# Rotating 96 planes by 180 degrees: all transfers on one DMA ring, in 8 MB pieces

The program runs on one core of a Trainium2 chip. The metric is the device time of one execution in microseconds (us), as a median of several executions; the other core of the pair is idle, so every bandwidth below is that of a single core.

Some words first. HBM is the main memory, in which input and output lie; SBUF is the core's working memory. A DMA transfer moves data between them, or within one of them, and is cut into packets. A ring is the queue in which the transfers of one issuing engine wait for the DMA engines. A transfer has landed when its last semaphore record is in.

## The reference

```python
def setup_inputs():
    batch, c, h, w = 32, 3, 256, 256
    return {"x": np.random.randn(batch, c, h, w).astype(np.float32)}

def reference(x):
    return np.rot90(x, k=2, axes=(-2, -1)).astype(np.float32)
```

Each of the 96 planes of 256 x 256 floats is read backwards, element by element. 25.17 MB come in, 25.17 MB go out, and nothing is computed.

## The kernel before

The planes are worked on in three groups of 32. In a group each plane is cut into four rows of 64 KB, so a group fills a tile of 128 partitions x 64 KB, 8.39 MB. VectorE reverses the elements within a row; the store reverses the order of the four rows (`::-1`). Three tiles of 64 KB per partition are in use: groups 0 and 2 are loaded to A and reversed into Ct, group 1 is loaded to Bt and reversed in place with the help of T.

```python
def load(t, g, lo=0, hi=E):
    nc.sync.dma_start(out=t[:, lo:hi], in_=x4[g][:, lo:hi])

def store(t, g):
    for lo in (0, E // 2):
        nc.scalar.dma_start(out=o4[g][:, ::-1, lo:lo + E // 2],
                            in_=t[:, lo:lo + E // 2])
...
load(A, 0)
load(Bt, 1)
across(Ct, A)      # 4 copies, 8.9 us
store(Ct, 0)
load(A, 2)
inside(Bt)         # 12 copies, 15.1 us
store(Bt, 1)
across(Ct, A)
store(Ct, 2)
```

SyncE (SP) issues the loads and ScalarE (ACT) the stores, so there are two rings of DMA work, and the 16 DMA engines serve both.

## Time and profile before

| | before |
|---|---|
| device time, median of 3 | 123.26 us |
| profiled execution | 123.51 us, span 121.7 us |
| VectorE busy | 32.5 us (27%) |
| DMA engines busy, SP's ring and ACT's ring | 49.3% + 47.9% |
| bytes over the span | 50.33 MB, 413 GB/s |

The lines themselves stand in the prediction. A share of "16 engines" is the sum of the durations of the packets that *start* in the stretch asked for, over 16 times the length of the stretch; in a short stretch it may pass 100%. The time of one packet follows by dividing.

### The profile page before, as it was taken

To read this page: it belongs to the slowest core of one execution; us is meant where nothing else is said; L and a number is where in the kernel's file an instruction comes from. 1 tells how busy PE (TensorE), PEld (TensorE's weight loads), DVE (VectorE), ACT (ScalarE), POOL (GpSimd) and SP (SyncE) were. 2 spreads that over 40 slices of the span, in tenths; PEclk is the share of its full clock that TensorE was granted. 3 is DMA by queue.
4 is the path that set the end of the run, shared out by engine and by line. 5 is a ranking of instruction groups with operands and counts; after the bars stand their busy time and mean duration, and the time that the engine had idled before them with its cause. 6 is when DMAs were issued, how large, how long until landed. Compare 5 with 4: busy or idle time off the path is not lost.

```text
span 121.7 us, 78 instructions
## 1 busy us (share of the span) xinstructions
DVE 32.5 (27%) x20; POOL 0.2 (0%) x4
## 2 busy tenths in 40 slices
DVE  0000000599400000699992000199700000000000
POOL 0000000000000000000000000000000000000000
DMA  9779977998978999899998996999898989999992
GB/s 345 345 345 495 538 345 345 560 474 345 345 301 388 485 441 431 366 485 441 452 409 388 517 452 301 463 398 485 377 485 388 485 377 485 398 463 409 452 431 108
DMA packets 1296, 50.33 MB, mean 413 GB/s; under 512 B 144, under 2 KB 144, under 8 KB 144
## 3 DMA queue, kind: packets, MB, share of 16 engines
q1 hardware_dynamic: 432, 25.17, 49.3%
q10 hardware_dynamic: 864, 25.17, 47.9%
HBM read 25.17 MB, written 25.17 MB: 413 GB/s over the span
## 4 chain that ended last, share of the span: by engine, by line
DMA 57%; DVE 13%; DVEq 2%; issue 0%
DMA A<-in_x_dram 57%; DVE Ct L53 13%; DVEq L108 2%; DVEq L53 0%
## 5 line engine op out<-in xcount | busy, mean ns | idle before, releaser
L53 DVE COPY Ct<-A 128x4096 f32<-128x4096 f32 x8 | 17.8, 2288 | 36.8 <-DMA A<-in_x_dram 36.8
L53 DVE COPY T<-Bt 128x2048 f32<-128x2048 f32 x4 | 4.9, 1228 | 18.0 <-DMA Bt<-in_x_dram 17.9
L53 DVE COPY Bt<-T 128x2048 f32<-128x2048 f32 x4 | 4.9, 1227 | 0.1
L53 DVE COPY Bt<-Bt 128x2048 f32<-128x2048 f32 x4 | 4.9, 1226 | 0.1
L97 POOL MEMSET const-uint8-127<- 128x1 uint8 x1 | 0.1, 102 | 0.0
L97 POOL MEMSET const-bfloat16-1.0<- 128x1 bf16 x1 | 0.1, 101 | 0.0
L97 POOL MEMSET const-float32-0.0<- 128x1 f32 x1 | 0.1, 98 | 0.2 <-issue 0.2
L97 POOL MEMSET const-float32-1.0<- 128x1 f32 x1 | 0.1, 98 | 0.0
## 6 DMA issues: line engine op xcount, KB each, us to landing
out_dram<-Ct ACTq DMA_DIRECT2D x4, 4096.0 KB, 34.2
out_dram<-Bt ACTq DMA_DIRECT2D x2, 4096.0 KB, 32.6
A<-in_x_dram SPq DMA_DIRECT2D x2, 34.5
Bt<-in_x_dram SPq DMA_DIRECT2D x1, 48.4
```

Source lines behind the costliest of these rows:

```text
L53: tc.keep_in_program_order(nc.vector.tensor_copy(out=dst, in_=src))
L97: nc = _bacc.Bacc("TRN2", target_bir_lowering=False, num_devices=1)
L108: with _tile.TileContext(nc) as tc:
```

## The change

Its intent: no competition between the rings. Loads and stores go through SP's ring alone, in the order load, load, store, load, store, store, and every transfer is one of 8 MB in 64 KB packets, half as many store packets as before.

```diff
     def store(t, g):
-        for lo in (0, E // 2):
-            nc.scalar.dma_start(out=o4[g][:, ::-1, lo:lo + E // 2],
-                                in_=t[:, lo:lo + E // 2])
+        nc.sync.dma_start(out=o4[g][:, ::-1, :], in_=t[:, :])
```

## The prediction

> **What bounds the kernel now.** I read the page first (engines, DMA row, queues, chain), then the issues in order of time, then the queue lines of three stretches, and last the packet records of the trace one by one. The page:
>
> ```profile
> DVE 32.5 (27%) x20; POOL 0.2 (0%) x4
> ...
> DMA  9779977998978999899998996999898989999992
> ...
> DMA packets 1296, 50.33 MB, mean 413 GB/s; under 512 B 144, under 2 KB 144, under 8 KB 144
> ...
> q1 hardware_dynamic: 432, 25.17, 49.3%
> q10 hardware_dynamic: 864, 25.17, 47.9%
> ...
> DMA A<-in_x_dram 57%; DVE Ct L53 13%; DVEq L108 2%; DVEq L53 0%
> ```
>
> VectorE works 27% of the span, the DMA engines 49.3 + 47.9 = 97.2%. q1 is SP's ring with the loads (25.17 MB in 64 KB packets), q10 is ACT's with the stores (25.17 MB in 32 KB packets); the small packets are semaphore writes. The chain of waits names a load for 57% and VectorE for 13%, but it stops at VectorE's last copy, at 87.6 us. The 34 us after that are stores draining, which the chain does not follow. So I trust the queue lines and not the chain: the bound is the 16 DMA engines, and the question is how many microseconds of them are not spent at full pace.
>
> The issues in order of time (start, length, engine, what):
>
> ```profile
> 0.73 0.37 SPq L56 DMA_DIRECT2D A<-in_x_dram  x1
> 1.15 0.42 SPq L56 DMA_DIRECT2D Bt<-in_x_dram  x1
> 22.80 8.90 DVE L53 COPY Ct<-A 128x4096 f32<-128x4096 f32 x4 [22.80 <-DMA A<-in_x_dram]
> 27.32 4.96 ACTq L60 DMA_DIRECT2D out_dram<-Ct  x2
> 31.72 0.33 SPq L56 DMA_DIRECT2D A<-in_x_dram  x1
> 49.61 1.23 DVE L53 COPY T<-Bt 128x2048 f32<-128x2048 f32 x1 [17.91 <-DMA Bt<-in_x_dram]
> ```
>
> From 27.3 us on both rings hold work, and each takes a share: the second load lands only at 49.6 and the third at 78.6 us (landing 46.9 us after its issue), against 22.0 us for the first, which had the engines alone.
>
> Queue lines of three stretches, 29 to 37 us, 37 to 77 us, and 80 to 118 us (name: packets, MB, share of 16 engines' time):
>
> ```profile
> q1 hardware_dynamic: 40, 2.62, 92.8%
> q10 hardware_dynamic: 20, 0.66, 19.0%
> ```
> ```profile
> q1 hardware_dynamic: 192, 10.88, 62.8%
> q10 hardware_dynamic: 203, 6.13, 35.5%
> ```
> ```profile
> q10 hardware_dynamic: 568, 16.52, 100.6%
> ```
>
> Divide time by packets. In the mixed stretch 10.88 MB are 166 load packets; 62.8% of 16 x 40 us is 401.9 us, so 2.42 us each (27.1 GB/s an engine, 434 GB/s for 16). 6.13 MB are 187 store packets of 1.21 us each, the same pace. Stores alone, third stretch: 504 packets in 611.6 us, 1.21 us again. The packet records agree: median 2.418 us for 64 KB and 1.213 us for 32 KB, whether the other ring runs or not. Only the first stretch differs: 40 load packets share 118.8 us, 2.97 us each. Loads and stores together cost nothing; the *arrival* of the stores at 29 us does. Summed over the records, load packets begun from 29 to 37 us take 1.38 us per engine beyond the median, those begun before 4 us (the very first) 0.57 us, all later ones 0.
>
> **What the Trainium skill says.** "DMA: Bandwidth & Descriptors", section "Issuing engines are not separate DMA queues": DMAs started by different engines run on the same 16 DMA engines and interleave; using several issuers saves only issue time. The trace agrees: 434 GB/s with one ring and with two, and an issue takes 0.33 to 0.62 us. The same page, section "Queues, rings and completion order": each engine takes turns between the rings that have work, a packet at a time. Agrees: a 64 KB load packet against a 32 KB store packet would share engine time 2 to 1, and the mixed stretch has 62.8 to 35.5. "Where 436 GB/s comes from", same page, gives 435 GB/s as the ceiling of the 16 ports; the records' 434 is that, so no order of transfers can raise the steady pace. "HBM Reference", section "Latency", gives an HBM access of 0.2 us on average and 2 us at high load; no row here isolates it, and I use it only for the size of one rival below.
>
> **The change part by part.**
>
> 1. *ACT issues nothing; six 4 MB stores become three 8 MB stores of 64 KB packets.* If a 64 KB store packet takes what a 64 KB load packet takes, 2.418 us, then 24 of them per engine (384 over 16) take 24 x 2.418 = 58.03 us, against 48 x 1.213 = 58.22 us now: 0.19 us saved. Fewer semaphore packets (9 ns each in the records, three fewer per engine): 0.03 us, neglected.
>
> 2. *One ring, strictly in order: load 0, load 1, store 0, load 2, store 1, store 2.* Each is 8 packets per engine, 8 x 2.418 = 19.34 us. Load 0 lands at 22.8 as now. Then load 1 at 42.1, store 0 at 61.5, load 2 at 80.8, store 1 at 100.1, store 2 at 119.5. I must check that each is in the ring before the ring runs dry. Store 0 is issued when the copy ends at 31.7 (now its first half goes at 27.3; SP has to wait for all of it); load 2 right after, at about 32.3: both before 42.1. Load 1 lands 7.5 us earlier than now, and the in-place reversal (12 copies, 49.61 to 64.7, so 15.1 us) runs from 42.2 to 57.3; store 1 is issued then, before the ring empties at 80.8. Load 2 lands at 80.8, Ct has been free since 61.5, the copies (8.9 us) end at 89.8; store 2 is issued at about 90, ten microseconds before 100.1. The ring never empties after 1.7 us, and all 32.5 us of VectorE stay hidden. SP's waits are in the order in which they come true, so no load is held behind a store that could have gone first in a harmful way.
>
> 3. *The end.* Now the last store lands at 120.94 (semaphore records) and the span ends 0.79 us later. Replayed with full-pace packets from load 0's landing, today's kernel would end at 22.77 + 16 x 2.418 + 48 x 1.213 = 119.68; it ends at 120.94, so 1.26 us on the slowest engine are the disturbance at 29 to 37 us. With the change and no disturbance: 22.77 + 40 x 2.418 = 119.49, span 120.28. Saving 1.26 + 0.19 = 1.45 us. The timed runs lie 123.26 - 121.73 = 1.53 us above the span, which I keep: 121.8 us at best.
>
> **The rivals.**
>
> *A. The disturbance belongs to waking a second ring.* For: it occurs when ACT's ring gets its first work, the very first packets on SP's ring also run long (2.69 to 3.47 us for most), and the issues at 63.5, 64.7, 83.2 and 87.6 us, which find a ring still filled, show no long packet. Then it goes with the second ring: 121.8 us.
>
> *B. It belongs to the first stores of the run, whichever ring carries them.* For: the same moment is also the first write to HBM. Then it returns at about 41 us: 121.8 + 1.3 = 123.1 us. The trace cannot separate A and B; I give A 60%.
>
> *C. One ring pays for every change of direction.* With two rings an engine switches between load and store at nearly every packet at no cost, which speaks against it. But each ring may read ahead while the other writes; in one ring, a load behind a store might first have to fetch. There are three changes of direction. If each stalls for a latency between the skill's 0.2 and 2 us, an estimate from that page, it is 0.6 to 6 us; with the free switching seen I expect 0.1 us each, 0.3 in sum.
>
> *D. SP's strict order starves the ring.* Part 2 leaves 9 to 23 us of room at every issue, so this needs an error of 9 us in my schedule: hardly possible.
>
> *E. The earlier landing of loads 1 and 2 speeds the kernel.* Load 1 does land 7 us earlier, but nothing that ends late waits for it: worth 0.
>
> **Range and chances.** 121.8 + 0.4 x 1.3 (B) + 0.3 (C) = 122.6; C may well be zero, so I put 122.4 us, 0.7% faster than 123.26. Low end 121.5: A, and a slightly better start. High end 123.5: B, with some of C. Faster by over 2% means under 120.8, a span under 119.3; even the 48 packets per engine at 2.418 us (116.06) plus the first packet's start at 1.73 and the 0.79 at the end give 118.6, without the long first packets and the spread of the engines. That needs an error in the packet time: 3%. Slower by over 2% means over 125.7, so 4 us of stalls that only C at its upper size gives: 4%. Within 2%: 93%.
>
> **What would show each step.** The queue line of the page should have one ring with about 50.33 MB, about 97 to 98% of the engines' span, and no q10; the packets fall to some 864 (768 of 64 KB and 96 semaphore writes). Landings near 22.8, 42, 61.5, 81, 100 and 119.5 us prove the FIFO schedule; steps clearly over 19.4 us show where the loss is. Rival B shows as long packets around 41 us; C as idle engines or long packets at 41, 61 and 80 us alike; D as an issue on SP after its predecessor has landed. VectorE's first copy of the in-place reversal should start near 42 instead of 49.6 us. I am wrong if 64 KB store packets take more than 2.42 us, if direction changes stall, or if the end after the last landing grows.

## The result

| | before | after |
|---|---|---|
| device time, median | 123.24 us (4 runs, 123.02 to 123.27) | 123.14 us (4 runs, 123.04 to 123.27) |
| ratio, 95% interval | | 0.9997 (0.998 to 1.0014) |
| span of the profiled execution | 121.73 us | 121.26 us |

A ratio is the mean time of one kernel's fast runs over that of the other's of the same rounds, so not quite the ratio of these medians. The change made no difference that can be told from zero; a later repetition of five rounds (below) says the same.

The page of the changed kernel, with the lines that answer to those of before:

```profile
DVE 32.5 (27%) x20; POOL 0.2 (0%) x4
...
DMA packets 864, 50.33 MB, mean 415 GB/s; under 512 B 96, under 2 KB 96, under 8 KB 96
...
q1 hardware_dynamic: 864, 50.33, 97.3%
```

One ring, 864 packets, 97.3% of the engines' time: as busy as before. The issues and copies in order of time (start, length, engine, what, and in brackets what VectorE waited for):

```profile
22.57 8.90 DVE L53 COPY Ct<-A 128x4096 f32<-128x4096 f32 x4 [22.57 <-DMA A<-in_x_dram]
31.50 0.63 SPq L59 DMA_DIRECT2D out_dram<-Ct  x1
32.17 0.59 SPq L56 DMA_DIRECT2D A<-in_x_dram  x1
43.09 1.23 DVE L53 COPY T<-Bt 128x2048 f32<-128x2048 f32 x1 [11.62 <-DMA Bt<-in_x_dram]
...
58.22 0.55 SPq L59 DMA_DIRECT2D out_dram<-Bt  x1
81.94 8.90 DVE L53 COPY Ct<-A 128x4096 f32<-128x4096 f32 x4 [23.74 <-DMA A<-in_x_dram]
90.86 0.54 SPq L59 DMA_DIRECT2D out_dram<-Ct  x1
```

The schedule is the foretold one, an issue always well before its turn. From the semaphore records, the six transfers land at 22.55, 43.07, 62.60, 81.84, 101.17 and 120.46 us. The steps between them are 20.5, 19.5, 19.2, 19.3 and 19.3 us: all are the 8 x 2.418 = 19.34 us of eight full-pace packets, but for the first, which is 1.2 us too long. Where those 1.2 us are, the queue line of two stretches of 2 us shows, 38.5 to 40.5 us (the last packet of load 1 on each engine) and 77.5 to 79.5 us (the last packet of load 2):

```profile
q1 hardware_dynamic: 16, 1.05, 177.1%
...
q1 hardware_dynamic: 16, 1.05, 121.5%
```

With 16 packets begun in 2 us, one on each engine, the mean packet is the share times 2 us: 3.54 us in the first stretch, 2.43 us in the second. 120.9% would be the undisturbed 2.418 us. So the last load packet before store 0 takes 1.12 us more, on all 16 engines (0.89 to 1.55 in the packet records), and the last one before store 1, which also goes from loading to storing, takes what any packet takes. I call these 1.1 us the toll. (The records do not name the engine of a packet; but the end of one packet is the start of the next, and so they fall into 16 rows of equal length.) In the kernel before it was 1.38 us: ten engines lost 1.1 to 1.4 us in the load packet ahead of their first store packet, six lost 0.6 to 0.8 us there and another 0.7 to 1.1 us in the next load packet.

### The profile page after: what moved, and what is told of

Read it like the earlier page. It is cut to its first block, busy times and chain, and to the rows that moved or that the text cites. A ratio compares the mean times of both kernels' runs of the same rounds, so it can differ in the third digit from the quotient of the medians.

```text
span 121.3 us, 72 instructions
## 1 busy us (share of the span) xinstructions
DVE 32.5 (27%) x20; POOL 0.2 (0%) x4
## 3 DMA queue, kind: packets, MB, share of 16 engines
q1 hardware_dynamic: 864, 50.33, 97.3%
## 4 chain that ended last, share of the span: by engine, by line
DMA 59%; DVE 13%; DVEq 2%; SPq 1%; issue 0%
DMA A<-in_x_dram 59%; DVE Ct L53 13%; DVEq L106 2%; SPq L59 1%; DVEq L53 0%
```

## The experiments

In all that follows *excess* is the time of packets beyond the usual 2.418 us (64 KB) or 1.213 us (32 KB), summed and divided by 16 engines; the start's excess of 0.5 to 0.8 us is in nearly every run (0.3 us in the run that begins with a copy) and left out unless named. Runs given with a ratio were timed in five rounds. All others (the four with extra transfers, the one with 1 KB rows, the two on eight engines, and the four under "What pays it") were executed once, so from them only the packet times within that execution are read. Theory B after the result: the toll comes with the first stores. Theory A, which the result already speaks against: it comes with a second ring. The diffs are against the changed kernel.

**The two parts of the change alone.** First one ring, but stores in halves:

```diff
-        nc.sync.dma_start(out=o4[g][:, ::-1, :], in_=t[:, :])
+        for lo in (0, E // 2):
+            nc.sync.dma_start(out=o4[g][:, ::-1, lo:lo + E // 2],
+                              in_=t[:, lo:lo + E // 2])
```

> One ring as in the changed kernel, but every store as two 4 MB transfers of 32 KB packets. Theory B (the first stores of a run cost about 1.1 us per engine once, whatever ring and size they have): the last load packet before store 0 again runs long, near 39 us, by 1.0 to 1.3 us per engine; nothing long near 60 and 80 us; 48 store packets of 1.213 us make the span 0.2 us longer than the changed kernel's 121.26, so 121.4 to 121.6. Rival A (a second ring's waking): no long packets at all, span near 120.4; the changed kernel has already spoken against it. Rival F (it is the 64 KB size of the store packets that costs): no long packets near 39 us here, span near 120.3.

Then whole 8 MB stores, but on ACT's ring (`nc.scalar.dma_start` in place of `nc.sync.dma_start`):

> Two rings as in the kernel before, but every store as one 8 MB transfer of 64 KB packets. Store 0 now goes at 31.7 us instead of 27.3. Theory B: long load packets right after 32.5 us, 1.1 to 1.4 us per engine, then none; the rings share the engines 1 to 1 where both have work; span 121.2 to 121.7, the same as before within 0.3%. Rival A, as far as it still stands beside B (both a ring's waking and the first store cost something): 1.5 us per engine or more.

Measured: halves on one ring 123.51 us, ratio to the kernel before 1.0028 (0.9989 to 1.0066); whole stores on two rings 123.52 us, 1.0039 (0.9993 to 1.0085). Neither part differs from before by more than the noise, and neither hides a gain that the other takes back. The last load packets before store 0, one ring with halves, 38.4 to 40.4 us:

```profile
q1 hardware_dynamic: 16, 1.05, 169.5%
```

And two rings with whole stores, 33 to 35 us:

```profile
q1 hardware_dynamic: 16, 1.05, 182.8%
```

3.39 and 3.66 us a packet: the toll is 0.97 and 1.24 us, with either ring and either size of packet. Theory F of the expectation (the packet size) falls, and A with it. Two departures: the halves also lost 0.46 us in small pieces between 25 and 37 us, and their profiled execution was a long one (124.59 us), in which one engine lost 0.42 us more near 62 us and 0.77 us near 80 us. In the run with whole stores another 0.23 us were lost near 74 us. Such stalls of single engines show in other runs too, and single executions of one kernel lie up to 1.5 us apart on these chips; I did not find their cause.

**Is it the first store?** A small store of zeros to the first output region (128 rows of 512 B, overwritten later), from ACT at the start or on SP's ring between loads 0 and 1:

```diff
+    nc.vector.memset(Z[:, :], 0.0)
     load(A, 0)
+    nc.scalar.dma_start(out=o4[0][:, ::-1, :128], in_=Z[:, :])   # or nc.sync
     load(Bt, 1)
```

> The changed kernel and one small store more (64 KB of zeros to the first output region, 512 B rows, overwritten later), issued by ACT right at the start, beside load 0. Theory B in the form 'once per run': the long packets near 39 us are gone (excess under 0.1 us per engine there); the first packets, which are long anyway, may take up to 1.1 us more, or nothing if the two waits overlap. Span 120.2 to 121.3. If the cost belongs to the change from load to store in a ring that has only loaded so far, or to the first large store: the long packets near 39 us stay at 1.1 us and the span is 121.3 or more.

> The same small store, but on SP's ring between load 0 and load 1, so that it is done at about 21 us in the middle of loading. Theory B, once per run: the long packets move from 39 us to about 19 to 22 us, load 0 lands up to 1.1 us later (23.7 instead of 22.6), none near 39 us; span as the changed kernel's, 121.2 to 121.5. If the cost belongs to the first large store: long packets stay near 39 us.

Measured: 123.49 us, 1.0006 (0.9974 to 1.0038), and 123.48 us, 1.0012 (0.9986 to 1.0038). Of the run with the store between the loads, the stretches 19 to 21 us and 38 to 40.5 us:

```profile
q1 hardware_dynamic: 16, 1.05, 121.1%
...
q1 hardware_dynamic: 16, 1.05, 143.5%
```

2.42 us, then 143.5% of 2.5 us, 3.59 us. The toll did not move, in either run (1.22 us near 39 us in the other). So the first write to the output is not what costs: that small store landed 0.2 us after load 0. "The first stores of the run", theory B in my first wording, was wrong as well, or at least too wide.

**Size, target and source.** Now a larger transfer between loads 0 and 1, from a part of Ct that a memset has filled; it is 2 MB (16 KB rows) to the output, to a scratch tensor in HBM, or within SBUF, and 512 KB (4 KB rows) to the output:

```diff
+    nc.vector.memset(Ct[:, :4096], 0.0)
     load(A, 0)
+    nc.sync.dma_start(out=o4[0][:, ::-1, :4096], in_=Ct[:, :4096])
+    # or out=S[:, :] in HBM, or out=Ct[:, 8192:12288], or 1024 columns to o4[0]
     load(Bt, 1)
```

> The changed kernel with one extra 2 MB store (16 KB rows of zeros, to the first output region, overwritten later) on SP's ring between load 0 and load 1: about 4.9 us more traffic. Theory B1 (the run's first store of some size costs about 1.1 us per engine once, in the load packet before it or in its own first packets): the excess moves to about 19 to 24 us and is gone before store 0 (then near 43 to 44 us). Theory B2 (only the switch to the first 8 MB store, whatever was stored before): about 1.1 us stays near 43 to 44 us, and nothing near 20 us. Span about 126.1 under both.

> The same extra store, but into a scratch tensor in HBM instead of the output. If it is the first large write to HBM anywhere (B1): the same picture as with the output, excess near 20 us, none near 43 us. If it belongs to the addresses of the output (B3): about 1.1 us stays near 43 us.

> The same extra transfer, but from SBUF to SBUF, so that DMA engines read SBUF in bulk and write no HBM. If the first large DMA read of SBUF costs (B4): excess near 20 us, none near 43 us. If the first large HBM write costs (B1): none near 20 us and about 1.1 us near 43 us.

> The extra store cut to 512 KB (4 KB rows): 1.2 us more traffic. The 64 KB store of 512 B rows moved nothing. Under B1 the size at which the cost moves lies between: here either most of the 1.1 us moves to about 20 us (then a store this small is enough), or it stays near 40 us (then it is not), or it splits in proportion.

The last packets of load 0, 19 to 21 us, and the stretch with the last packets of load 1, for the 2 MB copy within SBUF (second stretch 43 to 46 us):

```profile
q1 hardware_dynamic: 16, 1.05, 171.3%
...
q1 hardware_dynamic: 16, 1.05, 80.6%
```

and for the 512 KB store (second stretch 38 to 43 us, 32 packets):

```profile
q1 hardware_dynamic: 16, 1.05, 170.4%
...
q1 hardware_dynamic: 32, 2.10, 96.7%
```

In the copy 3.43 us, then 80.6% of 3 us, 2.42 us. In the 512 KB store 3.41 us, then 96.7% of 5 us over two packets each, 2.42 us. In all four the toll moved to the load packet ahead of the extra transfer (1.27 us for the output, 1.21 for the scratch tensor, 1.01 within SBUF, 0.99 for 512 KB), and before store 0 at most 0.23 us was left. A copy that writes no HBM pays it, so it is the *source* in SBUF, or the pause in the HBM reads, and not the write. The spans (126.7, 126.6, 126.0 and 123.0 us) are the changed kernel's plus the extra traffic, to within 0.6 us: the toll is paid once, here or there, and an early payment wins nothing.

A smaller rung, the copy within SBUF with 1 KB rows, between loads 0 and 1:

> A rung of the size ladder: an SBUF-to-SBUF copy of 128 KB (1 KB rows, 8 packets per engine) on SP's ring between load 0 and load 1. 512 B rows (to HBM) moved none of the cost, 4 KB rows all of it. Either about 1 us moves to near 20 us (then 8 KB per engine is enough), or it stays near 39 us.

In the source this copy stands before load 0; the issues, at 0.73, 1.17 and 1.75 us, have it between load 0 and load 1. The last packets of load 1, 38.4 to 40.4 us:

```profile
q1 hardware_dynamic: 16, 1.05, 173.3%
```

3.47 us: the toll stayed near 39 us (1.05 us), and 0.06 us appeared near 20 us. So 8 KB per engine in 1 KB packets did not pay, and 32 KB per engine in 4 KB packets (the 512 KB store) did. The two differ in the size of the packets too, and this was not tested apart.

**Paying it beside the long first packets.** If the toll overlapped with the start's own 0.65 us, an early copy from ACT would beat both kernels. The copy is within SBUF, with 4 KB or 2 KB rows:

```diff
+    nc.vector.memset(Ct[:, :1024], 0.0)      # or 512
     load(A, 0)
+    nc.scalar.dma_start(out=Ct[:, 8192:8192 + 1024], in_=Ct[:, :1024])
     load(Bt, 1)
```

> The changed kernel with an SBUF-to-SBUF copy of 512 KB (4 KB rows of a memset part of Ct) issued by ACT at about 2 us, beside the start of load 0. Theory B4 (the first DMA reads of SBUF in bulk cost about 1 us per engine once): nothing long is left near 39 us. If the cost overlaps with the long first load packets (0.65 us per engine), total excess falls from 1.8 to about 1.0, the copy itself costs 1.3 us, and the span is 121.3 to 121.8; if it does not overlap, total excess stays 1.7 to 1.9 and the span is 122.3 to 122.8. Rival (the cost is tied to the first store): about 1.1 us stays near 40 us, span 122.5.

> The same with 2 KB rows, 256 KB, issued about half a microsecond earlier. Copy costs about 0.65 us. If 2 KB rows are enough and the cost overlaps with the start: span 120.8 to 121.1, a little faster than both kernels; enough but no overlap: 121.8; not enough: about 1.1 us stays near 40 us, span 121.9.

Neither is faster: 124.22 us, 1.0093 (1.0073 to 1.0113), and 123.60 us, 1.0035 (1.0021 to 1.005). These two are clearly slower, by about the copies' own traffic. The last packets of load 1 in the run with 4 KB rows, 39.8 to 41.8 us:

```profile
q1 hardware_dynamic: 16, 1.05, 180.2%
```

3.60 us: the toll is still there. But the overlap itself was not tested: in the packet records the first copy packets begin at 7.0 us, when each engine had two load packets behind it and its long first one had ended. Nor did the copies pay later. On ACT's ring eight 4 KB packets per engine went out, most of them one at a time between 64 KB load packets; those of the 512 KB store on SP's ring went out in a row, and they paid. So not the amount read from SBUF seems to count, but an unbroken stretch of it. The two runs differ in ring and target as well, but the kernel before and the run with whole stores on ACT's ring fit: there a single store packet of 32 or 64 KB stood between two load packets, and the toll was paid.

**Each engine's own?** A copy within SBUF that only 8 engines carry, one 32 KB packet each, between loads 0 and 1. The first attempt used rows 0 to 7:

```diff
+    nc.vector.memset(Ct[:8, :8192], 0.0)
     load(A, 0)
+    nc.sync.dma_start(out=Ct[:8, 8192:], in_=Ct[:8, :8192])
     load(Bt, 1)
```

> The changed kernel with an SBUF-to-SBUF copy of 8 rows of 32 KB between load 0 and load 1, which goes to 8 of the 16 engines, one packet each. If the cost is each engine's own: 8 long packets of about 1.1 us near 20 us and 8 near 40 us. If it is one event for the whole memory or fabric: long packets near 20 us and none near 40 us. If an engine needs several packets to have paid it: 16 near 40 us.

It was a poor probe that taught something. The copies took 3.20 to 3.84 us, 3.43 us on average, in place of 1.21. The Trainium skill, "DMA: Bandwidth & Descriptors", section "The descriptor swizzle", gives partitions 0 to 3 and 4 to 7 one port each, so eight rows met at two ports; the 3.43 us agree with that in kind, not in size: four rows that take turns at one port would need 4 x 1.21 = 4.85 us, an estimate from that page's ports. And the eight engines without a copy stalled too, each for 3.3 us in the packet it began near 22 us; the eight with a copy lost 1.1 us more in the load packet behind it, so all 16 lost 3.3 us. After this no engine paid a toll before store 0; the stretch 39 to 44 us has 2.42 us a packet:

```profile
q1 hardware_dynamic: 32, 2.10, 96.9%
```

So eight engines that had read nothing from SBUF were spared, after a stall. The second attempt put the rows on partitions 0, 4, ... 28 (`Ct[0:32:4, ...]`), eight different ports by the same section, and the copies took the full-pace 1.213 us:

> The copy on 8 engines between load 0 and load 1 again, but with its 8 rows on partitions 0, 4, ... 28, in the hope that they do not meet at the same few SBUF ports (then 1.3 us for a packet, not 3.4). If each engine pays its own toll: 8 long load packets of about 1 us near 19 us, and 8 of about 1.1 us near 39 us. If it is one event for all: 16 near 19 us and none near 39 us. If one packet is not enough: 16 near 39 us.

The stretches 19 to 21 us and 39 to 41 us:

```profile
q1 hardware_dynamic: 16, 1.05, 157.8%
...
q1 hardware_dynamic: 16, 1.05, 144.2%
```

3.16 us and 2.88 us: all 16 engines lost 0.74 us when 8 of them turned to SBUF, and all 16 lost another 0.47 us when the whole set did. None of the three forecasts fits. In this run the toll is charged to all engines together, in parts, as the engines make the switch; together it is 1.2 us. The kernel before also has it in parts, but not evenly (six engines lost 1.6 us on average, ten 1.3).

**What pays it, what keeps it.** Four more runs. An empty ring near 22 us, by letting load 1 wait until load 0 has landed; a copy from HBM to HBM in place of the 512 KB store; the 512 KB copy within SBUF ahead of load 0; and an empty ring near 62 us.

```diff
     load(A, 0)
+    copy(Bt[:, :1], A[:, :1])                                     # h1: load 1 waits
+    nc.sync.dma_start(out=S[:, :], in_=x4[2][:, :1024])           # h2: HBM to HBM
     load(Bt, 1)
...
+    copy(Ct[:, :1], Bt[:, :1])                                    # k1: after store 0,
+    copy(A[:, :1], Ct[:, :1])                                     #     load 2 waits
     load(A, 2)
```

(Each run has one of these. The third, h3, has the memset and the copy within SBUF before `load(A, 0)`, with the order of the issues fixed.)

> The changed kernel, but load 1 is issued only after load 0 has landed (one column of Bt is first written from A), so that SP's ring runs dry for 2 to 3 us near 22 us. If any pause in the HBM reads pays the toll of about 1.1 us: none is left near 41 to 44 us, and only the restart near 24 us is long (like the start, 0.6 us). If only packets that read SBUF pay it: the toll of about 1.1 us stays near 41 to 44 us. Span 121.3 plus about 3.

> The changed kernel with a 512 KB copy from HBM to HBM (4 KB rows) on SP's ring between load 0 and load 1, the twin of the 512 KB store there, which moved the toll to about 20 us. If it is the source in SBUF that pays: no excess near 20 us beyond the copy's own length, about 1.1 us stays near 40 us. If it is a write to HBM that pays as well: about 1 us near 20 us, none near 40 us.

> The 512 KB SBUF-to-SBUF copy ahead of load 0 on SP's ring, so that the run begins with packets that read SBUF. If it is the first bulk read of SBUF: the toll is paid at the start or not visible there, none near 41 us; total excess 0.6 to 1.8 us. If it is the first change from a stretch of HBM reads to a stretch of SBUF reads, whatever came before: about 1.1 us stays near 41 us.

The empty ring near 22 us did not pay: it cost a restart, 0.65 us of long packets, and the toll came near 41 us all the same. The stretch 40 to 42 us:

```profile
q1 hardware_dynamic: 16, 1.05, 184.7%
```

3.69 us, a toll of 1.28 us. The copy from HBM to HBM, stretches 19 to 21 us and 39.3 to 41.3 us:

```profile
q1 hardware_dynamic: 16, 1.05, 120.9%
...
q1 hardware_dynamic: 16, 1.05, 164.9%
```

2.42 us, then 3.30 us: it paid nothing, though it has the size and the HBM target of the 512 KB store that paid. So the source in SBUF is needed. The copy within SBUF ahead of load 0, stretch 41 to 43 us:

```profile
q1 hardware_dynamic: 16, 1.05, 190.5%
```

3.81 us: a stretch of SBUF reads *before* any load pays nothing; the toll, 1.39 us, is still to come. It is not "the first bulk read of SBUF" but the first switch *from* loading *to* it.

> The changed kernel, but load 2 is issued only after store 0 has landed (through one column copied over Ct), so that the ring runs dry for 2 to 3 us near 62 us. The toll near 39 us stays, 1.1 us. In the kernel without the pause the second switch from loading to storing, near 80 us, is free. If the toll buys a state that lives only while the engines are kept busy (theory S), the pause loses it, and a second toll of about 1.1 us appears near 81 to 84 us; total excess 3.5, span about 125.5. If it is paid once per run whatever follows, nothing is long near 84 us: total excess 2.5, span about 124.2.

With the ring empty near 62 us, the stretches 38.4 to 40.4, 63 to 66 and 81.2 to 83.2 us:

```profile
q1 hardware_dynamic: 16, 1.05, 181.1%
...
q1 hardware_dynamic: 16, 1.05, 105.5%
...
q1 hardware_dynamic: 16, 1.05, 181.1%
```

3.62 us, a restart at 105.5% of 3 us, 3.17 us, and 3.62 us once more. The second switch, free in the changed kernel (121.5% in such a stretch, above), now costs 1.2 us like the first. In this one execution, then, the toll bought a state that lasted through later loads and stores while the ring had work, and was gone once the ring had run empty (for 1.8 to 3.2 us, engine by engine): once per unbroken stretch of work, not once per run.

**The changed kernel again**, in five rounds:

> The changed kernel once more, unaltered, timed in five rounds to settle the sign: the packets save 0.19 us, the toll differs by 0.2 to 0.3 us in the profiles, so a ratio of 0.996 to 1.000 is expected under theory B; the prediction's best case (toll gone) would be 0.988.

123.25 us against 123.34 us of the kernel before, ratio 1.0016 (0.9982 to 1.005); one execution of six took 124.46 us and lifts the mean. The sign stays open; the foretold best case, 0.988, lies outside the interval, and so does the foretold 0.7% (0.993).

## Why the prediction was wrong

The prediction was 122.4 us, 0.7% faster, in a range of 121.5 to 123.5; measured were 123.14 us, inside the range, and a gain that cannot be told from zero. The mechanism of the schedule was right, the gain was not there.

- *The bound and the packet times*: right. 64 KB store packets take 2.418 us as foretold; the ring is never empty and VectorE stays hidden (D and E: nothing, as foretold). The 0.19 us of part 1 is there in the packet records but too small for the timed runs.
- *Part 3, the 1.26 us of disturbance, and the 60% for rival A*: this step failed. With no second ring the toll came back, 1.12 us of the 1.38, moved from 29 to 37 us to the moment when the first ring turns from load 1 to store 0. The evidence that I used for A was right but misread: the issues at 63.5 us and later show no long packet; by the later runs this is because the toll had been paid in that stretch of work, and not because their ring was awake.
- *Rival B, 1.3 us*: the size was right (1.12), the reason only in part. A small first store does not pay, a copy that stores nothing in HBM does.
- *Rival C, 0.3 us for three changes of direction*: zero after the first. Near 60 and 80 us the excess is 0.03 us or less; in the repetition it was 0.02 and 0.08 us.
- *The constant between span and device time*: I took 123.26 - 121.73 = 1.53 us, the median of three runs minus the span of another, longer execution. Taken within one execution it is 1.78 us, so the best case should have read 120.28 + 1.78 = 122.06, not 121.8. Add the toll of 1.12: 123.18 us, against 123.14 measured.

What the toll is inside stays open. The runs show: it comes when loads from HBM are followed by a stretch of packets that read SBUF (32 KB per engine were enough, 8 KB in 1 KB packets were not); with three different targets it was the same within 0.3 us; it falls on the load packet before the stretch; in the run with the copy on eight different ports all engines shared it; in the other run on eight engines it was gone after the stall of 3.3 us; in one execution it was due again after the ring had run empty. No record here separates the reads from the writes of a packet, and so no run says why the switch costs.

No version that I tried beats both kernels.

## What to carry to other kernels

When the queue lines say 97% and the packets run at their full pace, moving transfers between rings cannot gain more than the sum of the long packets, so list those one by one and ask which of them the change removes. A long packet that appears when a second ring starts is not yet the second ring's: here the same one appeared in a single ring, at its first turn from loading to storing. Keep the ring from running empty, for here a pause cost itself, a restart of about 0.7 us, and this toll again.

## What the Trainium skill lacked or had wrong

- No page has the toll: the first turn from HBM loads to an unbroken stretch of SBUF reads cost 0.9 to 1.4 us on all 16 engines, once per stretch of uninterrupted DMA work as far as one run with a pause shows. It would belong to "DMA: Bandwidth & Descriptors", section "Latency and other measured facts".
- The same page, section "Where 436 GB/s comes from", says in its warning that for HBM to SBUF the HBM side, about 358 GB/s, binds. One core alone ran at the pace of 434 GB/s here, loads (64 KB in 2.418 us on each of 16 engines) and stores alike; the page's own 425 GB/s and "HBM Reference" are nearer.
- No page says of a local copy that engines without a part in it can stall with it ("DMA: Bandwidth & Descriptors", section "Back-pressure in remote DMA", has this for remote transfers, for engines that share a path): eight engines lost 3.3 us beside a copy of eight rows on partitions 0 to 7 that others carried, and 16 lost 0.74 us beside a copy with distinct ports.
- No page says that the first 64 KB packets of an empty ring are long: they took 0.5 to 0.8 us more, at the start and after each pause. The same page has a latency to the first byte of a transfer; whether that is the same thing no run here shows.
